# The order of TensorE's seven products per K pair: the products with t2 and t3 behind that with b22

## The chip, the cores and the metric

The kernel runs on one core of one Trainium2 chip. The metric is the device time of one execution in microseconds (us). The engines named below are TensorE (PE in the profile; PEld is its weight load, one ahead of each matmul), VectorE (DVE), ScalarE (ACT), GpSimd (POOL) and SyncE (SP, which only issues DMAs here).

## The reference

A trunk of two layers on x of 1 x 256 x 2048, in float32. Each layer is an attention part with two kinds of heads and a SwiGLU part, each between two RMS norms:

```python
for l in range(DEPTH):
    h = rms_norm(x, pre_mix_norm[l])
    m = hybrid_mixer(h, l, w_in[l], w_o[l], ...)     # h @ w_in, two attentions, @ w_o
    x = x + rms_norm(m, post_mix_norm[l])
    h = rms_norm(x, pre_ffn_norm[l])
    f = (silu(h @ w_gate[l]) * (h @ w_up[l])) @ w_down[l]
    x = x + rms_norm(f, post_ffn_norm[l])
```

w_in is 2048 x 6144, w_o 2048 x 2048, w_gate and w_up 2048 x 5632, w_down 5632 x 2048. The work around the change is these dense products of 256 tokens with the weights.

## The kernel before, in words

**Precision.** Each float32 operand is split into hi (rounded by ScalarE, line 307 or 279) and lo = value - hi (a subtraction on VectorE, line 317 or 281, for some weights on GpSimd, line 310). One product of two blocks is three matmuls into one PSUM bank: hi x hi, hi x lo, lo x hi (`product`, lines 1083 to 1086; a matmul there moves 512 columns against a stationary 128 x 128).

**Tiling.** K is walked in pairs (kp) of 2 x 128 rows, tokens in two halves of 128, columns in blocks of 512. For a pair and two blocks of columns the plain form needs eight block products, that is 24 matmuls (line 1250 in gate/up, lines 1356 to 1359 in down). In selected pairs the kernel uses a form with seven products instead (`seven_products`), 21 matmuls: sums of token blocks (s1 to s4, from `token_sums`) meet sums of weight blocks (t1 to t4), and four banks p1, p6, p7, q5 collect parts which `shared_part` (lines 1125 to 1129) adds to the four result banks at the end.

**How the sums of weights come about.** `mixed_weights` does it for each such pair from two weight tiles, G and T (T arrives with the first half of G added by an accumulating DMA of GpSimd, line 258). In program order: split of the whole T tile, which gives t1 and b22 together (hi on ScalarE, lo on VectorE, 128 x 1024); then on VectorE T<-T (line 290, 128 x 512: t2) and G<-G,T (line 291, 128 x 1024: t3 and t4); then the splits of t2 (Th<-T, Tl<-T, 128 x 512) and of t3 and t4 together (Th<-G, Tl<-G, 128 x 1024). In the profile's names, hi and lo of t1 and b22 are `hi` and `lo`, those of t2, t3 and t4 are `Th` and `Tl`.

**Where it is used.** In gate/up (eleven chunks c of 512 columns for each layer, eight pairs each) with two to five sevens in a chunk: chunk 0 has two, 1 has three, 2 and 10 four, 3 to 9 five, in the order kp 0, 2, 1, 3, 4, 5, 6, 7 with 2, 3, 4, 5, 6 as sevens. In down, in seven pairs of each half. In the input projection, pairs 4 and 5 of four of six column pairs, and in the output projection two pairs of its second half.

**What sets the order.** A scheduler places the instructions of each engine from the program order, priorities and its own estimate of when operands and buffers are ready; TensorE's matmuls, too, may stand elsewhere than the text has them. Each engine then runs its list in that order and waits at each instruction for what it needs. hi and lo have six buffers each, plain weight tiles (raw) four, G three, T four in gate/up; an instruction that fills a buffer waits for the last reader of its old content. SP issues the weight loads in one queue.

Of the kernel before, what the change touches and what calls it, by code (L numbers as in the profile page):

```python
# [167 lines left out]
def kernel(  # L168
# [30 lines left out]
    def four_banks(odd, names):  # L199
        makers = (bank, bank, bank, last_bank) if odd else (acc_bank,) * 4  # L200
        return [make(n) for make, n in zip(makers, names)]
# [143 lines left out]
    def weights(i, ahead):  # L345
        feed(i + 1 + ahead)
        return ready[i]
# [198 lines left out]
    def tick():  # L546
        clock[0] += 1
        for e in list(running):
            if e[0] <= clock[0]:
                try:  # L550
                    n = next(e[1])
                    e[0] = clock[0] + (PACE if n is None else n)
                except StopIteration:
                    running.remove(e)
# [508 lines left out]
    def seven_in(banks, extra, sums, xT, l, cc, kp, first, last):  # L1063
        hi, lo = weights(plan[l]["in"][cc[0], kp], LOOKAHEAD)
        m = weights(plan[l]["in"][cc[1], kp], LOOKAHEAD)
        seven_products(banks, extra, sums, *pair_blocks(xT, kp), hi, lo, m, first, last)
# [14 lines left out]
    def product(a, stat, moving, first, last):  # L1081
        sh, sl = stat
        hi, lo = moving
        nc.tensor.matmul(a, sh, hi, start=first, stop=False, skip_group_check=open_sums[0])  # L1084
        nc.tensor.matmul(a, sh, lo, start=False, stop=False, skip_group_check=open_sums[0])  # L1085
        return nc.tensor.matmul(a, sl, hi, start=False, stop=last, skip_group_check=open_sums[0])  # L1086
# [18 lines left out]
    def seven_products(banks, extra, sums, a11, a12, a22, hi, lo, m, first, last):  # L1105
        s1, s2, s3, s4 = sums
        p1, p6, p7, q5 = extra
        todo = (
            (p1, a11, (hi[:, 0, :], lo[:, 0, :]), first, last),
            (banks[0], a12, (hi[:, 1, :], lo[:, 1, :]), False, False),  # L1110
            (q5, s1, m["t1"], first, last),
            (p7, s3, m["t3"], first, last),
            (p6, s2, m["t2"], first, last),
            (banks[1], s4, m["b22"], False, False),
            (banks[2], a22, m["t4"], False, False),
        )
        for n, job in enumerate(todo):
            if n % 2 == 0:
                tick()
            newest_seven[0] = product(*job)  # L1120
# [14 lines left out]
    for l in range(L):  # L1135
# [27 lines left out]
        for kp in LATE_O:  # L1163
            i, j = (plan[l]["o"][c, kp] for c in (2, 3))
            if kp not in O_SEVEN:
                for c, i in ((2, i), (3, j)):
                    unit({t: accs[c, t] for t in range(NT)}, mix, i, kp, range(NT), kp == LATE_O[0], False)
                continue
            if kp == O_SEVEN[0]:
                extra = four_banks(False, [f"{q}_o{l}" for q in ("p1", "p6", "p7", "q5")])  # L1170
            hi, lo = weights(i, LOOKAHEAD)
            m = weights(j, LOOKAHEAD)
            seven_products(got, extra, forms[kp], *pair_blocks(mix, kp), hi, lo, m, kp == O_SEVEN[0], kp == O_SEVEN[-1])
            if kp == O_SEVEN[-1]:
                for t in range(NT):
                    mg[t, 1] = pool.tile([P, 2, CW], F32, tag="qk", bufs=4, name=f"mg_o{l}_{t}_1")
                shared_part(extra, [mg[t, 1][:, h, :] for t in range(NT) for h in range(2)])
                for c in (2, 3):
                    nc.vector.tensor_tensor(out=accs[c, 1], in0=accs[c, 1], in1=mg[1, 1][:, c - 2, :], op=shared_sign(1, c - 2))
# [72 lines left out]
        def seven(banks, extra, c, kp, first, last):  # L1252
            hi, lo = weights(plan[l]["gate"][c, kp], LOOKAHEAD)
            m = weights(plan[l]["up"][c, kp], LOOKAHEAD)
            e, o = xT[2 * kp], xT[2 * kp + 1]
            a11, a12, a22 = (e[:, 0, 0:P], e[:, 1, 0:P]), (o[:, 0, 0:P], o[:, 1, 0:P]), (o[:, 0, P:S], o[:, 1, P:S])
            seven_products(banks, extra, forms[kp], a11, a12, a22, hi, lo, m, first, last)

        for c in range(FF // CW):
            banks = four_banks(1 - c % 2, [f"c{q}_{l}_{c}" for q in ("11", "12", "21", "22")])  # L1260
# [62 lines left out]
        for half in range(2):  # L1323
# [74 lines left out]
            for t in range(NT):  # L1398
# [4 lines left out]
                for c in cc:  # L1403
                    for kp in range(nkp - tail, nkp):
# [4 lines left out]
                        for kk in range(2):  # L1409
                            sh, sl = jh[:, kk, t * P : (t + 1) * P], jl[:, kk, t * P : (t + 1) * P]  # L1410
                            last = kp == nkp - 1 and kk == 1
# [63 lines left out]
```

## Time and profile before

| | |
|---|---|
| median of 3 runs | 2189.1 us (2187.52 to 2189.52) |
| the profiled execution | 2189.0 us, of which its span is 2187.3 us |
| granted TensorE clock | 0.999 of full speed |
| ScalarE hi<-raw, 128 x 1024 | 494 times, mean 1055 ns |
| VectorE lo<-raw, 128 x 1024 | 472 times, mean 1221 ns |
| VectorE G<-G,T | 124 times, mean 1219 ns |
| DMA | 470.96 MB, mean 215 GB/s |

How to read it: the profile is of one execution. Busy times of TensorE come from modelled ends, and neighbouring instructions overlap, so the distance between starts tells more than the busy share. A line of a time line gives start, length, engine, source line, operation, out<-in and shape, and in brackets the idle time before it with what ended it. A line of the view of waits gives who waited for whom, the sum, the count and the longest. Gate/up runs from about 395 to 850 us in layer 0 and from about 1483 to 1940 us in layer 1.

### The profile page before, as it was taken

To read this page: it belongs to the slowest core of one execution; us is meant where nothing else is said; L and a number is where in the kernel's file an instruction comes from. 1 tells how busy PE (TensorE), PEld (TensorE's weight loads), DVE (VectorE), ACT (ScalarE), POOL (GpSimd) and SP (SyncE) were. 2 spreads that over 40 slices of the span, in tenths; PEclk is the share of its full clock that TensorE was granted. 3 is DMA by queue.
4 is the path that set the end of the run, shared out by engine and by line. 5 is a ranking of instruction groups with operands and counts; after the bars stand their busy time and mean duration, and the time that the engine had idled before them with its cause. 6 is when DMAs were issued, how large, how long until landed. Compare 5 with 4: busy or idle time off the path is not lost.

```text
span 2187.3 us, 28757 instructions
## 1 busy us (share of the span) xinstructions
PE 2170.0 (99%) x9950; PEld 1782.2 (81%) x9950; DVE 1914.1 (88%) x2639; ACT 1393.4 (64%) x2083; POOL 251.1 (11%) x241
## 2 busy tenths in 40 slices
PE   9999999999999999999999999999999999999998
PEld 7888888788888888888878888887888888888886
DVE  7888658999999999989878886589999999999997
ACT  7666665766666656666665656657566666666664
POOL 2100000031221220000010000001212212200000
PEclk9999999999999999999999999999999999999999
DMA  9545554587887876767465555555878877767683
GB/s 324 194 163 174 192 189 168 184 291 234 243 261 222 234 228 228 231 216 255 146 241 174 181 176 182 193 170 184 292 226 255 249 222 231 239 216 233 207 265 101
DMA packets 140563, 470.96 MB, mean 215 GB/s; under 512 B 15984, under 2 KB 17008, under 8 KB 139904
## 3 DMA queue, kind: packets, MB, share of 16 engines
q1 hardware_dynamic: 121952, 436.03, 57.7%
q0 software_dynamic: 17888, 32.55, 8.9%
q8 instruction: 78, 1.28, 0.2%
q10 hardware_dynamic: 576, 0.54, 0.1%
q14 instruction: 69, 0.57, 0.1%
HBM read 460.67 MB, written 8.39 MB: 214 GB/s over the span
## 4 chain that ended last, share of the span: by engine, by line
PE 87%; DVE 7%; issue 2%; DMA 2%; ACT 1%; SPq 0%; DVEq 0%; ACTq 0%
PE c L1250 16%; PE in L1084 7%; PE in L1086 7%; PE in L1085 7%; PE dn L1356 4%; PE dn L1357 4%; PE dn L1359 4%; PE p L1085 2%; PE c L1086 2%; PE c L1084 2%; PE c L1085 2%; PE p L1086 2%; PE p L1084 2%; PE o L569 2%; PE o L570 2%
## 5 line engine op out<-in xcount | busy, mean ns | idle before, releaser
L317 DVE TENSOR_TENSOR lo<-raw,hi 128x1024 fp32r<-128x1024 f32 x472 | 567.8, 1221 | 99.0 <-ACT hi L307 97.9
L307 ACT ACTIVATE hi<-raw 128x1024 fp32r<-128x1024 f32 x494 | 509.8, 1055 | 144.2 <-PE c L1086 36.8
L1250 PE MATMUL c<-hi,xF 128*128 128x512 f32 x1280 | 346.0, 391 | 0.1
L1250 PEld LDWEIGHTS c<-hi,xF 128*128 128x128 f32 x1280 | 238.3, 188 | 49.1 <-DVE xF L493 0.6
L258 POOL DMA_DIRECT2D T<-in_weights_in_turn_dram x124 | 108.8, 877 | 1343.6 <-DMA T<-in_weights_in_turn_dram 764.8
L1250 PE MATMUL c<-lo,xF 128*128 128x512 f32 x640 | 198.2, 390 | 2.5 <-DVE lo L317 2.5
L1356 PE MATMUL dn<-hi,jh 128*128 128x512 f32 x432 | 168.2, 389 | 0.0
L1357 PE MATMUL dn<-lo,jh 128*128 128x512 f32 x432 | 168.1, 389 | 0.0
L307 ACT ACTIVATE hi<-G 128x1024 fp32r<-128x1024 f32 x124 | 131.1, 1057 | 52.1 <-DMA G<-in_weights_in_turn_dram 20.8
L281 DVE TENSOR_TENSOR Tl<-G,Th 128x1024 fp32r<-128x1024 f32 x124 | 151.2, 1220 | 14.5 <-ACT Th L279 14.5
L279 ACT ACTIVATE hi<-T 128x1024 fp32r<-128x1024 f32 x124 | 130.3, 1051 | 51.0 <-PE c L1086 29.8
L279 ACT ACTIVATE Th<-G 128x1024 fp32r<-128x1024 f32 x124 | 130.8, 1055 | 47.8 <-DVE G L291 47.5
L281 DVE TENSOR_TENSOR lo<-T,hi 128x1024 fp32r<-128x1024 f32 x124 | 156.5, 1262 | 2.9 <-ACT hi L279 2.4
L291 DVE TENSOR_TENSOR G<-G,T 128x1024 f32<-128x1024 f32 x124 | 151.2, 1219 | 2.1
L1250 PEld LDWEIGHTS c<-lo,xF 128*128 128x128 f32 x640 | 120.1, 188 | 28.2 <-DVE lo L317 3.0
L317 DVE TENSOR_TENSOR lo<-G,hi 128x1024 fp32r<-128x1024 f32 x106 | 129.2, 1219 | 12.2 <-ACT hi L307 12.0
L1359 PE MATMUL dn<-hi,jl 128*128 128x512 f32 x432 | 133.0, 389 | 0.0
L1084 PE MATMUL in<-hi,xT 128*128 128x512 f32 x328 | 131.4, 402 | 0.5 <-ACT hi L889 0.5
L279 ACT ACTIVATE Th<-T 128x512 fp32r<-128x512 f32 x124 | 78.2, 631 | 83.6 <-DVE T L290 82.9
L1084 PE MATMUL in<-hi,xI 128*128 128x512 f32 x328 | 131.1, 401 | 0.0
L1085 PE MATMUL in<-lo,xI 128*128 128x512 f32 x328 | 128.0, 390 | 0.3 <-DVE lo L317 0.3
L1086 PE MATMUL in<-hi,xI 128*128 128x512 f32 x328 | 127.9, 391 | 0.0
(485 smaller groups left out, 4917.7 us busy)
## 6 DMA issues: line engine op xcount, KB each, us to landing
raw<-in_weights_in_turn_dram SPq DMA_DIRECT2D x494, 512.0 KB, 4.6
T<-in_weights_in_turn_dram SPq DMA_DIRECT2D x124, 512.0 KB, 5.5
G<-in_weights_in_turn_dram SPq DMA_DIRECT2D x124, 512.0 KB, 5.6
T<-in_weights_in_turn_dram POOLq DMA_DIRECT2D x124, 256.0 KB, 5.7
GU<-in_weights_in_turn_dram SPq DMA_DIRECT2D x32, 512.0 KB, 6.2
V<-in_weights_in_turn_dram SPq DMA_DIRECT2D x8, 512.0 KB, 3.9
away_ffn<-x SPq DMA_DIRECT2D x8, 512.0 KB, 7.4
xd<-away_ffn SPq DMA_DIRECT2D x8, 512.0 KB, 9.5
```

What stands on the lines that cost most here:

```text
L279: nc.scalar.activation(h, w, AF.Copy)
L281: newest_rest[i] = nc.vector.tensor_tensor(out=l, in0=w, in1=h.bitcast(F32), op=ALU.subtract)
L291: nc.vector.tensor_tensor(out=g, in0=g, in1=t2.unsqueeze(1).to_broadcast([P, 2, CW]), op=ALU.add)
L307: nc.scalar.activation(hi, raw, AF.Copy)
L317: rest = nc.vector.tensor_tensor(out=lo, in0=raw, in1=hi.bitcast(F32), op=ALU.subtract)
L1084: nc.tensor.matmul(a, sh, hi, start=first, stop=False, skip_group_check=open_sums[0])
L1085: nc.tensor.matmul(a, sh, lo, start=False, stop=False, skip_group_check=open_sums[0])
L1086: return nc.tensor.matmul(a, sl, hi, start=False, stop=last, skip_group_check=open_sums[0])
L1250: nc.tensor.matmul(a, stat[part], w[j][:, kk, :], start=first and kk + n == 0, stop=last and kk == 1 and n == 2)
L1356: nc.tensor.matmul(accs[c, t], sh, hi[:, kk, :], start=first, stop=False, skip_group_check=open_sums[0])
L1357: nc.tensor.matmul(accs[c, t], sh, lo[:, kk, :], start=False, stop=False, skip_group_check=open_sums[0])
L1359: nc.tensor.matmul(accs[c, t], sl, hi[:, kk, :], start=False, stop=last, skip_group_check=open_sums[0])
```

## The change

In `seven_products` the list of seven products is put in another order. Before, q5 (t1) is followed by p7 (t3), p6 (t2), banks[1] (b22) and banks[2] (t4); after, by banks[1], p6, p7 and banks[2]. The products themselves, their banks and their first and last marks stay.

```diff
             (q5, s1, m["t1"], first, last),
+            (banks[1], s4, m["b22"], False, False),
+            (p6, s2, m["t2"], first, last),
             (p7, s3, m["t3"], first, last),
-            (p6, s2, m["t2"], first, last),
-            (banks[1], s4, m["b22"], False, False),
             (banks[2], a22, m["t4"], False, False),
```

Because the scheduler works from this order, the lists of ScalarE, VectorE and SP change in places as well; GpSimd's list is the same.

## The prediction

> **What bounds the kernel now.** I read the page first, then busy times by stretches, then who waits for whom on the weight-load queue (PEld), then time lines of one chunk.
>
> ```profile
> span 2187.3 us, 28757 instructions
> PE 2170.0 (99%) x9950; PEld 1782.2 (81%) x9950; DVE 1914.1 (88%) x2639; ACT 1393.4 (64%) x2083; POOL 251.1 (11%) x241
> ```
>
> TensorE bounds it, but its 99% is made of modelled ends that overlap. What TensorE loses must be read from the starts of the weight loads: one precedes each matmul. The time line of one stalled pair (gate/up chunk 4 of layer 0, kp 5), from the last load of q5:
>
> ```profile
> 594.28 0.19 PEld L1086 LDWEIGHTS q<-hi,sl 128*128 128x128 f32 x1
> 594.51 0.41 PEld L1084 LDWEIGHTS p<-Th,sh 128*128 128x128 f32 x2
> 594.96 0.19 PEld L1085 LDWEIGHTS p<-Tl,sh 128*128 128x128 f32 x1
> 595.19 0.19 PEld L1086 LDWEIGHTS p<-Th,sl 128*128 128x128 f32 x1
> 595.42 0.19 PEld L1084 LDWEIGHTS c<-hi,sh 128*128 128x128 f32 x1
> 595.64 0.19 PEld L1085 LDWEIGHTS c<-lo,sh 128*128 128x128 f32 x1
> 596.25 0.19 PEld L1085 LDWEIGHTS p<-Tl,sh 128*128 128x128 f32 x1 [0.42 <-DVE Tl L281]
> 596.36 0.19 PEld L1086 LDWEIGHTS p<-Th,sl 128*128 128x128 f32 x1
> 596.60 0.19 PEld L1086 LDWEIGHTS c<-hi,sl 128*128 128x128 f32 x1
> ```
>
> Undisturbed starts stand 0.227 us apart (594.96 to 595.64: three steps, 0.68). From 595.64 to 596.60 there are three steps in 0.96, so this stall cost 0.28, which is its idle time of 0.42 less 0.14: 0.04 is the gap between any two loads, 0.10 is caught up by the next load at 596.36. The order seen is already not the one in the text: the scheduler has put p7's Tl product behind p6's three and two of b22's, and it still waits. All such waits:
>
> ```profile
> PEld p L1085 <- DVE Tl L281: 11.3, 20, 1.2
> PEld p L1084 <- ACT Th L279: 2.1, 6, 0.7
> PEld p_in L1085 <- DVE Tl L281: 0.4, 1, 0.4
> ```
>
> That is 13.8 us idle in 27 places, so 13.8 - 27 x 0.14 = **10.0 us** of lost TensorE time: the most that this change can remove. The Trainium skill (TensorE: Matmul & The Clock Gate, section "Architectural detail: the array is 16x 32x32, not 1x 128x128") says that TensorE's queue can pull weight loads ahead of matmuls in flight; if that hid these waits the 10.0 would be nothing. The trace shows only 0.10 per stall caught up, so the rest counts.
>
> The second engine is near its end too. One chunk, then the sum over 14 of them (chunks 3 to 9 of both layers):
>
> ```profile
> 643.60:684.80 41.20, 41.20 (x187) 33.98 (x186) 40.10 (x45) 26.75 (x32) 9.24 (x7) 1.00 0.78 237
> sum 582.00, PE 578.60 PEld 475.35 DVE 560.69 ACT 373.67 POOL 125.78; mean PE 41.33 PEld 33.95 DVE 40.05 ACT 26.69 POOL 8.98
> ```
>
> The columns are stretch, length, then PE, PEld, DVE, ACT, POOL. A chunk takes 582.0/14 = 41.57 on average, of which VectorE works 40.05. The one shown runs in 41.20 at a granted clock of 1.00: that is about what TensorE needs.
>
> **The change, part by part.** No instruction is added or removed; in each of 144 pairs (96 of gate/up, 28 of down, 16 of the input and 4 of the output projection) the six matmuls of p6 and p7 let the three of b22 pass, and p7 lets p6 pass. What the pair needs is made in the order t1 and b22 (one split), t2, then t3 and t4 (one split). The new order of use, t1, b22, t2, t3, t4, is that order. Three effects follow.
>
> *First, TensorE asks later.* The built order (in which the scheduler places the instructions on each engine; it holds no times) after q5 is now b22 x3, p6 x3, p7 x3. Counted in places after q5's last load, the first Th product goes from place 1 to 4, which is 3 x 0.227 = 0.68 later. Where the scheduler had deferred p7's Tl product (chunks 3 to 9) it goes only from 7 to 8, 0.23 later; where it had not (chunk 1), from 5 to 8.
>
> *Second, VectorE's built order changes with it.* Its time line for the same pair, before:
>
> ```profile
> 592.64 0.68 DVE L281 TENSOR_TENSOR Tl<-T,Th 128x512 fp32r<-128x512 f32 x1
> 593.25 0.68 DVE L290 TENSOR_TENSOR T<-T 128x512 f32<-128x512 f32 x1
> 593.85 1.22 DVE L317 TENSOR_TENSOR lo<-raw,hi 128x1024 fp32r<-128x1024 f32 x1
> 594.98 1.22 DVE L281 TENSOR_TENSOR Tl<-G,Th 128x1024 fp32r<-128x1024 f32 x1
> 596.12 1.22 DVE L291 TENSOR_TENSOR G<-G,T 128x1024 f32<-128x1024 f32 x1
> 597.26 0.68 DVE L281 TENSOR_TENSOR Tl<-T,Th 128x512 fp32r<-128x512 f32 x1
> 597.86 2.35 DVE L317 TENSOR_TENSOR lo<-raw,hi 128x1024 fp32r<-128x1024 f32 x2
> 600.13 1.22 DVE L281 TENSOR_TENSOR Tl<-G,Th 128x1024 fp32r<-128x1024 f32 x1
> ```
>
> The stalled product waited for the Tl that begins at 594.98 and ends at 596.2. In chunks 3 to 9 of the changed kernel the lo ahead of it (593.85) stands behind the next Tl<-T, and the two lo at 597.86 behind the last Tl<-G. Steps are 1.14 for 128x1024 (594.98 to 596.12) and 0.60 for 128x512. So Tl<-G can begin at 593.85 and end at 595.1; TensorE asks at 594.28 + 8 x 0.227 = 596.1. **The stall goes, with 1.0 us to spare.** What is late next? The three lo belong to kp 7 and to the next chunk; they end at about 597.9, 600.1 and 601.3, and kp 7 begins after 602. The shared part behind them begins when it did, because the sum of work ahead of it is the same.
>
> *Third, TensorE gives hi back six places earlier*, and this is what the second effect needs. ScalarE:
>
> ```profile
> 592.21 1.06 ACT L307 ACTIVATE hi<-raw 128x1024 fp32r<-128x1024 f32 x1 [1.03 <-PE c L1086]
> 593.18 1.04 ACT L279 ACTIVATE Th<-G 128x1024 fp32r<-128x1024 f32 x1
> 597.25 1.06 ACT L307 ACTIVATE hi<-raw 128x1024 fp32r<-128x1024 f32 x1 [1.56 <-PE c L1086]
> 598.22 1.04 ACT L279 ACTIVATE Th<-G 128x1024 fp32r<-128x1024 f32 x1
> ```
>
> Both hi<-raw wait for b22's last product, and the Th<-G that VectorE needs stands behind each. Released 6 x 0.227 = 1.36 earlier, the first hi starts about 1.0 earlier (ScalarE's own work ends 1.03 earlier), its Th<-G as soon as the G sum that ends where VectorE's row 592.64 begins is written and ends near 593.8. The second starts at 595.7, its Th<-G near 596.7 instead of 598.22. VectorE then idles nowhere.
>
> DMA issues: SP's built list has two G loads ahead of raw loads that they stood behind. A G waits for the Tl<-G above, which is earlier; the raw loads wait for the lo that moved, up to 2.9 later (593.85 to 596.7). They feed kp 1 of the next chunk, which stands 69 matmuls (24 + 24 + 21) or 15.7 us behind the start of kp 7. I cost this at nothing; the cover is that distance. POOL's list is unchanged. In the input and output projections one or two lo now stand inside the shared part, 1.14 each, so its banks return later: bounds 0 to 10 x 1.14 = 11.4 us; I take 0, because no wait of TensorE for these sums exceeds the row of 0.2 below. Down: no Tl row there waits at all, 0.
>
> ```profile
> PEld o L569 <- DVE o L1179: 0.3, 2, 0.2
> ```
>
> The sum, by groups of waits (same view, in windows; each line is us, times, longest):
>
> ```profile
> PEld p L1085 <- DVE Tl L281: 2.9, 6, 0.8
> PEld p L1085 <- DVE Tl L281: 4.2, 6, 1.0
> PEld p L1085 <- DVE Tl L281: 0.9, 2, 0.6
> PEld p L1084 <- ACT Th L279: 0.3, 1, 0.3
> PEld p L1085 <- DVE Tl L281: 1.3, 2, 1.0
> PEld p L1084 <- ACT Th L279: 0.6, 2, 0.3
> PEld p L1085 <- DVE Tl L281: 1.2, 1, 1.2
> PEld p L1084 <- ACT Th L279: 0.7, 1, 0.7
> PEld p L1085 <- DVE Tl L281: 0.2, 1, 0.2
> PEld p L1085 <- DVE Tl L281: 0.3, 1, 0.3
> PEld p L1084 <- ACT Th L279: 0.2, 1, 0.2
> ```
>
> - Chunks 3 to 8 (first line layer 0, second layer 1): 7.1 in 12, a loss of 7.1 - 12 x 0.14 = 5.4. All of it goes; the longest, 1.0, is under 1.14 + 0.23.
> - Chunks 1 and 2 (lines 3 and 4 layer 0, 5 and 6 layer 1): 3.1 in 7, loss 2.1. Th waits (0.3) fall under 0.68. Chunk 2's Tl has one lo fewer ahead (1.14) and goes. Chunk 1 keeps VectorE's order; its Tl product moves 0.68 against idle of 0.6 and 1.0, so about 0.3 stays. Gain 1.8.
> - Chunk 9 (lines 7 and 8 layer 0, 9 layer 1): 2.1 in 3, loss 1.7. The Th wait of 0.7 moves 0.68; the Tl wait of 1.2, after it, gains 1.14 + 0.23 but TensorE also comes 0.6 earlier, so about 0.2 stays. Gain 1.5.
> - Input projection 0.4, loss 0.3, moved six places: gain 0.3.
> - Chunk 0 (last two lines, layer 0; layer 1 has the same): 1.0 in 4, loss 0.4, stays: there p6's Tl is late, and it keeps its place.
>
> Sum: 5.4 + 1.8 + 1.5 + 0.3 = **9.0 us**. The profiled execution took 2189.0 (its span 2187.3 and 1.7 around it), the median of the runs is 2189.1: forecast **2180.0**.
>
> **Rivals.**
> *A, VectorE is the bound.* 40.05 of 41.57 is 96%, TensorE's loads 33.95 of 41.57 are 82%: a removed stall only shows up at the next product that reads a Tl, and the time stays near 2189. The Trainium skill (Perfetto Trace Analysis, section "Identifying the Most-Contended Engine") judges VectorE by occupancy and TensorE by its weight loads, which gives this result. Against it: the chunk of 41.20 has VectorE at 40.10, so 1.1 is free.
> *B, the place alone.* If VectorE's Tl does not come earlier, chunks 3 to 8 gain 0.23 in 11 stalls and 0.1 in the least, 2.6; with about 0.8 in chunk 9, 1.1 in chunk 1 and 0.3 in the input, 4.8: 2184.2. This is also the case that the text's order does little because the scheduler had made it already.
> *C, slower: VectorE starves behind ScalarE.* If ScalarE's two Th<-G kept their times (end 594.2 and 599.3), VectorE, with the lo no longer ahead, would idle 0.45 and 0.95 more, 1.4 per chunk. A chunk would need 40.05 + 1.4 and 0.3 to 1.0 of its other idle time, 41.8 to 42.5: 0.2 to 0.9 over 41.57, in 14 chunks 3 to 13, less 2 gained elsewhere: 2190 to 2200, middle 2195. It decides at the second hi<-raw: C holds if it starts after 597, not at 595.7.
>
> **How the numbers follow.** A measurement tells about 0.2%, 4.4 us, from no change. Forecast (2178 to 2183) 0.58; B 0.14, half of it beyond 0.2%; A 0.11; C 0.13; 0.04 for more gain, as the whole 10.0 and earlier buffers. Faster 0.58 + 0.04 + 0.07 = 0.69, same 0.07 + 0.11 = 0.18, slower 0.13. The range takes in all but C and the lowest: 2177.5 to 2189.5.
>
> **What would show it.** Right: the Tl and Th waits of PEld fall from 27 to under 10, those of chunk 0 remain, Tl<-G stands ahead of the lo<-raw, and the 14 chunks take 41.2 each. Wrong: waits for lo at L1250 (lo moved too far), DVE idle before Tl<-G for ACT Th (C), or equal chunk times with new waits (A).

## The result and the profile after

| | before | after |
|---|---|---|
| median of 12 runs each, us | 2188.86 (2187.29 to 2190.99) | 2183.77 (2182.70 to 2185.63) |
| ratio, 95% interval | | 0.9976, 0.9968 to 0.9985 |
| span of the profiled execution, us | 2187.3 | 2181.9 |

The kernel is 5.1 us faster (5.4 between the two profiled spans); forecast were 9.0. The 2183.8 lies 0.8 above the 2178 to 2183 that had most of the chance, and inside the stated range only because that takes in rivals A and B as well. The first lines of the page after:

```profile
span 2181.9 us, 28776 instructions
PE 2166.4 (99%) x9950; PEld 1783.2 (82%) x9950; DVE 1913.6 (88%) x2639; ACT 1394.8 (64%) x2083; POOL 258.8 (12%) x241
```

Every engine runs as many instructions as before, and VectorE and ScalarE are busy as long to within 1.4 us. GpSimd is busy 7.7 longer, nearly all of it in its lo<-G (51.6 instead of 43.6); I have not followed that further. What changed above all are the waits. Whom TensorE's weight-load queue waited for after the change (us, times, longest):

```profile
PEld p L1085 <- DVE Tl L281: 2.7, 8, 0.8
PEld c L1250 <- DVE xF L493: 2.0, 2, 1.0
PEld pT_df L823 <- DVE w L1127: 1.9, 4, 0.6
PEld q L1084 <- DVE act L1309: 1.6, 4, 0.5
PEld p L1084 <- ACT Th L279: 0.4, 2, 0.2
```

The waits for Tl and Th fell from 13.8 us in 27 places to 3.1 in 10, and the one in the input projection is gone. The largest rows that are new or longer: TensorE now waits 2.0 for xF, the first operand of gate/up (before: 0.6 in 2), 1.9 for L1127 in the input projection, and 1.6 for a bank that VectorE evicts late (q).

Where the 5.4 went can be read from stretches. Gate/up, from its first weight load (L1250) to that of down, before and then after (stretch, length, then PE, PEld, DVE, ACT, POOL):

```profile
sum 927.60, PE 920.97 PEld 756.37 DVE 889.68 ACT 603.02 POOL 183.30; mean PE 460.48 PEld 378.19 DVE 444.84 ACT 301.51 POOL 91.65
```

```profile
395.75:855.00 459.25, 457.96 (x2063) 378.75 (x2064) 444.33 (x543) 302.41 (x386) 94.73 (x68) 1.00 0.76 236
1480.95:1941.68 460.73, 458.95 (x2063) 378.48 (x2064) 445.34 (x543) 301.95 (x386) 96.29 (x68) 1.00 0.77 237
sum 919.98, PE 916.91 PEld 757.24 DVE 889.67 ACT 604.36 POOL 191.02; mean PE 458.46 PEld 378.62 DVE 444.84 ACT 302.18 POOL 95.51
```

Gate/up gained 7.6 (927.60 to 919.98), and 2.2 were given back outside it. Its first load in layer 0 begins at 395.75 instead of 394.81, 0.9 later; and from the end of gate/up in layer 0 to its start in layer 1 it now takes 625.95 instead of 624.71, 1.2 longer.

**The pair that the prediction followed** (chunk 4 of layer 0, kp 5). VectorE and then TensorE, after:

```profile
593.13 0.69 DVE L290 TENSOR_TENSOR T<-T 128x512 f32<-128x512 f32 x1
593.74 1.23 DVE L281 TENSOR_TENSOR Tl<-G,Th 128x1024 fp32r<-128x1024 f32 x1
594.88 1.22 DVE L291 TENSOR_TENSOR G<-G,T 128x1024 f32<-128x1024 f32 x1
596.02 0.69 DVE L281 TENSOR_TENSOR Tl<-T,Th 128x512 fp32r<-128x512 f32 x1
```

```profile
593.61 0.19 PEld L1086 LDWEIGHTS q<-hi,sl 128*128 128x128 f32 x1
593.84 0.19 PEld L1084 LDWEIGHTS c<-hi,sh 128*128 128x128 f32 x1
595.20 0.19 PEld L1084 LDWEIGHTS p<-Th,sh 128*128 128x128 f32 x1
595.42 0.19 PEld L1085 LDWEIGHTS p<-Tl,sh 128*128 128x128 f32 x1
```

Tl<-G follows T<-T with no lo between, and p7's Tl product, eighth after q5's last load, is loaded at 595.42 without a wait. That Tl's row ends at 594.97, so some 0.45 are to spare. ScalarE, which decides about rival C:

```profile
592.65 1.06 ACT L279 ACTIVATE Th<-G 128x1024 fp32r<-128x1024 f32 x1 [0.63 <-DVE G L291]
593.93 0.63 ACT L279 ACTIVATE Th<-T 128x512 fp32r<-128x512 f32 x1 [0.23 <-DVE T L290]
594.47 1.99 ACT L307 ACTIVATE hi<-raw 128x1024 fp32r<-128x1024 f32 x2
596.37 1.04 ACT L279 ACTIVATE Th<-G 128x1024 fp32r<-128x1024 f32 x1
```

Neither hi<-raw waits for b22's last product any more, and the second Th<-G starts at 596.37 (596.7 forecast, 598.22 before).

**The hand-over from the output projection to gate/up.** ScalarE there, before and after:

```profile
381.43 1.06 ACT L307 ACTIVATE hi<-raw 128x1024 fp32r<-128x1024 f32 x1 [3.87 <-PE o L571]
```

```profile
382.35 1.06 ACT L307 ACTIVATE hi<-raw 128x1024 fp32r<-128x1024 f32 x1 [5.05 <-PE o L571]
```

This hi waits for a buffer that TensorE gives back, and it does so 0.92 later. VectorE's rows tell why, first before and then after (rows are left out at the dots):

```profile
376.64 1.23 DVE L317 TENSOR_TENSOR lo<-raw,hi 128x1024 fp32r<-128x1024 f32 x1
...
378.98 1.29 DVE L1179 TENSOR_TENSOR o<-o,mg_o 128x512 f32<-128x512 f32 x2
```

```profile
375.19 0.68 DVE L1126 TENSOR_TENSOR mg_o<-p_o,mg_o 128x512 f32<-128x512 f32 x1
375.79 1.21 DVE L317 TENSOR_TENSOR lo<-raw,hi 128x1024 fp32r<-128x1024 f32 x1
376.92 0.68 DVE L1127 TENSOR_TENSOR mg_o<-p_o,mg_o 128x512 f32<-128x512 f32 x1
377.52 1.22 DVE L317 TENSOR_TENSOR lo<-raw,hi 128x1024 fp32r<-128x1024 f32 x1
...
379.85 1.28 DVE L1179 TENSOR_TENSOR o<-o,mg_o 128x512 f32<-128x512 f32 x2
383.44 2.59 DVE L317 TENSOR_TENSOR lo<-raw,hi 128x1024 fp32r<-128x1024 f32 x2 [2.31 <-ACT hi L307]
```

Two lo<-raw now stand inside the shared part, where before one did, and the sums on the banks o_2_1 and o_3_1 (L1179) are ready 0.87 later. The scheduler therefore put nine products on the bank o_2_0 ahead of the twelve on o_2_1 and o_3_1, where before it put five (e8 tests that the two lo are the reason). The first of the twelve is loaded here, before and after:

```profile
379.73 0.19 PEld L569 LDWEIGHTS o<-hi,mix_sb 128*128 128x128 f32 x1 [0.15 <-DVE o L1179]
```

```profile
380.59 0.19 PEld L569 LDWEIGHTS o<-hi,mix_sb 128*128 128x128 f32 x1
```

The twelve end the use of two hi buffers, which come back 4 x 0.227 = 0.91 later; hi, lo, the sums of L589, x and xF are all later by that, and gate/up with them.

### The profile page after: what moved, and what is told of

Its sections match the earlier page's. It is cut to its first block, busy times and chain, and to the rows that moved or that the text cites. A ratio compares the mean times of both kernels' runs of the same rounds, so it can differ in the third digit from the quotient of the medians.

```text
span 2181.9 us, 28776 instructions
## 1 busy us (share of the span) xinstructions
PE 2166.4 (99%) x9950; PEld 1783.2 (82%) x9950; DVE 1913.6 (88%) x2639; ACT 1394.8 (64%) x2083; POOL 258.8 (12%) x241
## 3 DMA queue, kind: packets, MB, share of 16 engines
q8 instruction: 78, 1.28, 0.2%
## 4 chain that ended last, share of the span: by engine, by line
PE 92%; DVE 4%; ACT 2%; issue 1%; DMA 1%; SPq 0%; DVEq 0%; ACTq 0%
PE c L1250 18%; PE in L1084 7%; PE in L1086 7%; PE in L1085 7%; PE dn L1356 4%; PE dn L1357 4%; PE dn L1359 4%; PE p L1085 3%; PE c L1085 3%; PE p L1086 3%; PE c L1084 3%; PE c L1086 3%; PE p L1084 3%; PE o L569 2%; PE o L571 2%; PE o L570 2%
## 5 line engine op out<-in xcount | busy, mean ns | idle before, releaser
L1250 PE MATMUL c<-hi,xF 128*128 128x512 f32 x1280 | 345.8, 391 | 1.5 <-DVE xF L493 1.5
L1250 PEld LDWEIGHTS c<-hi,xF 128*128 128x128 f32 x1280 | 238.3, 188 | 50.3 <-DVE xF L493 2.0
L1250 PE MATMUL c<-lo,xF 128*128 128x512 f32 x640 | 198.1, 390 | 2.5 <-DVE lo L317 2.5
L1250 PEld LDWEIGHTS c<-lo,xF 128*128 128x128 f32 x640 | 120.1, 188 | 28.1 <-DVE lo L317 3.0
```

The source lines that it names most:

```text
L1250: nc.tensor.matmul(a, stat[part], w[j][:, kk, :], start=first and kk + n == 0, stop=last and kk == 1 and n == 2)
```

## The experiments

Theory 1: in gate/up the mechanism and sizes of the prediction hold, and the projections (input and output) give back what I costed at nothing. Rivals: B, the place alone does it (its 2184.2 lies nearest to the result); that VectorE's order alone does it; that the swap of t2 and t3 counts by itself. The kernel before was measured anew beside the experiments; its medians there lie between 2188.3 and 2189.5, so a difference between medians of two kernels is uncertain by about half a microsecond.

**The projections as before** (e1).

```diff
-            seven_products(got, extra, forms[kp], *pair_blocks(mix, kp), hi, lo, m, kp == O_SEVEN[0], kp == O_SEVEN[-1])
+            seven_products(got, extra, forms[kp], *pair_blocks(mix, kp), hi, lo, m, kp == O_SEVEN[0], kp == O_SEVEN[-1], True)
...
+        if old:
+            todo = todo[:3] + (todo[5], todo[4], todo[3]) + todo[6:]
```

(the call of the input projection likewise)

> The new product order in gate/up and down only; the input and output projections keep the order of before. Theory 1 (the projections give back time that the prediction costed at 0): between the changed kernel and this one the hand-over from the output projection to gate/up loses 0.89 and 0.91 in the two layers and the input projection 0.3 in each, less the 0.29 of the one stall that went there: 2.1 in all, so 2183.8 - 2.1 = 2181.7, within 2181.0 to 2182.5, and the matrix products of gate/up start when they did before (394.8). Rival 2 (the losses there are absorbed further on, or belong to where the trace was cut): the same as the changed kernel, 2183.8 within 0.5.

Measured 2181.64 (ratio to before 0.9965, 0.9953 to 0.9978), 2.1 under the changed kernel, as theory 1 has it (2.6, if each is taken against the kernel before beside it). By its trace the hand-over is back to its length of before, though this execution reached it later, so that gate/up starts at 396.48 and not at 394.8. Its gate/up, where every engine has the list of the changed kernel:

```profile
sum 918.60, PE 916.01 PEld 757.88 DVE 889.45 ACT 607.16 POOL 187.01; mean PE 458.01 PEld 378.94 DVE 444.72 ACT 303.58 POOL 93.51
```

That is a gain of 9.0 where the changed kernel's execution shows 7.6.

**Which lo: those of the hand-over held back** (e8). `held` is the kernel's own list that queues the next lo<-raw behind an instruction.

```diff
-                shared_part(extra, [mg[t, 1][:, h, :] for t in range(NT) for h in range(2)])
+                part = shared_part(extra, [mg[t, 1][:, h, :] for t in range(NT) for h in range(2)])
...
-                    nc.vector.tensor_tensor(out=accs[c, 1], in0=accs[c, 1], in1=mg[1, 1][:, c - 2, :], op=shared_sign(1, c - 2))
+                    part = nc.vector.tensor_tensor(out=accs[c, 1], in0=accs[c, 1], in1=mg[1, 1][:, c - 2, :], op=shared_sign(1, c - 2))
+                held[:] = part, 2
```

> The changed kernel, with the two lo<-raw that went into the output projection's shared part held behind its last sum (L1179). All else in VectorE's list is that of the changed kernel; the built order then puts the 12 products on o_2_1 and o_3_1 ahead of nine on o_2_0, so their hi come back 9 x 0.227 = 2.0 us earlier than in the changed kernel, 1.1 earlier than in before. Theory 1 (the hand-over is set by that return of hi: hi<-raw, lo, L589, L627, transposes, gate/up): gate/up starts at least 0.9 earlier than in the changed kernel in each layer, up to 2.0 if nothing else on the chain is late: 2183.8 - 1.8 = 2182.0 down to 2179.8. Rival 2 (the loss there comes from the product order itself, not from the lo): no change in the hand-over, 2183.8 within 0.7. Rival 3 (the held lo are late for o_3_0): waits for lo at L570 and a time above 2184.

Measured 2182.60 (0.9969, 0.9956 to 0.9981), 0.6 above theory 1's upper end. Its hand-over is as long as that of before, 0.9 shorter per layer than in the changed kernel. The profiled spans differ by 2.4 (2179.5 against 2181.9), the medians by 1.2. Here the product order is the new one and only the two lo moved, so the loss of the hand-over came through them. Why nothing beyond the state of before was gained, its trace tells:

```profile
380.48 1.07 ACT L307 ACTIVATE hi<-raw 128x1024 fp32r<-128x1024 f32 x1 [3.05 <-DVE lo L317]
```

```profile
384.56 0.69 DVE L589 TENSOR_TENSOR mg_o<-o,mg_o 128x512 f32<-128x512 f32 x1 [0.40 <-PE o L571]
387.28 0.69 DVE L589 TENSOR_TENSOR mg_o<-o,mg_o 128x512 f32<-128x512 f32 x1 [0.55 <-PE o L571]
```

The hi comes 1.9 earlier than in the changed kernel, but now waits for VectorE's lo, and L589 waits for the last products on o, which come later in turn. So two other limits stood just behind the first.

**Both together, the input projection as before** (e11): the call of the input projection takes the old order, the hold of e8 is added.

> New order in gate/up, down and the output projection, the two lo<-raw of its hand-over held behind its last sum; the input projection keeps the order of before. Theory 1 (the parts add): 2181.6 of the kernel with the projections as before, less 0 to 1.1 per layer from hi that comes back earlier than in before: 2179.4 to 2181.6. Rival 2 (the hand-over has another limit just behind, and gives nothing over before): 2181.6 to 2182.2.

Measured 2181.78 (0.9966, 0.9954 to 0.9979): in rival 2's range and 0.2 above theory 1's, no better than e1's 2181.64. These two are the best of the versions measured, 7.7 us under the kernel before.

**The place alone** (e7). The new order everywhere, but in chunks 3 to 8 VectorE's list is that of before; `then(a, b)` puts a behind b on their engine; TlG5, TlG6 are the Tl<-G of the pairs kp 5 and kp 6, lo_a, lo_b, lo_c the lo<-raw of gate kp 7, up kp 7 and the next chunk's first gate block. Not shown is a line that keeps the G<-G,T of kp 6 behind the Tl<-G of kp 5; this and the next two experiments have it.

```diff
...
+        if i in fifth:
+            done["TlG5"] = newest_rest[i]
+        if i in sixth:
+            done["TlG6"] = newest_rest[i]
...
+            if i in lo_a:
+                then(done["TlG5"], rest)
+            if i in lo_c:
+                then(done["TlG6"], rest)
```

> The new product order everywhere, but VectorE's order in chunks 3 to 8 of gate/up is that of before: each lo<-raw ahead of the Tl<-G. ScalarE's list is that of the changed kernel. Theory 1 (both effects are needed): at kp 5 the Tl<-G ends near 596.0 and p7 asks at 595.4, so a stall of about 0.6 comes back in most chunks, and the 12 stalls lose 2.8 to 7: 2186.6 to 2190. Rival 2 (the prediction's B, the place alone makes the gain; its 2184.2 was nearest to the result): the same as the changed kernel, 2183.8 within 0.7, without Tl waits in chunks 3 to 8.

Measured 2187.31 (0.9993, 0.9984 to 1.0002), in theory 1's range and 3.5 above the changed kernel: B's place is not what made the 2183.8. ScalarE's list in these chunks is that of the changed kernel, and so is TensorE's but for one place in each, at kp 6, where a product with t4 now stands ahead of p7's Tl. The Tl waits of TensorE, then two of them in chunk 4:

```profile
PEld p L1110 <- DVE Tl L281: 9.8, 26, 0.7
```

```profile
596.35 0.19 PEld L1110 LDWEIGHTS p<-Tl,sh 128*128 128x128 f32 x1 [0.36 <-DVE Tl L281]
601.49 0.19 PEld L1110 LDWEIGHTS p<-Tl,sh 128*128 128x128 f32 x1 [0.29 <-DVE Tl L281]
```

What the later place spares at kp 5, TensorE waits for at kp 6, whose Tl<-G ends when it did. The twelve chunks (3 to 8 of both layers) took 498.7, before 498.3: nothing gained, where B had 2.6. Rival A's words describe this case, a stall that only shows up at the next Tl.

**VectorE's order alone** (e6). The order of products of before; in chunks 3 to 8 each lo<-raw stands behind the Tl<-G, as in the changed kernel (TlT6 is the Tl<-T of kp 6). VectorE's list there is then that of the changed kernel. The scheduler answered with other lists for ScalarE and TensorE too, so VectorE's order is not the only thing that differs from the kernel before.

```diff
...
+            if i in lo_a:
+                then(rest, done["TlT6"])
+                then(done["TlG6"], rest)
+            if i in lo_b:
+                then(rest, done["TlG6"])
```

> The product order of before everywhere, but VectorE's order in chunks 3 to 8 of gate/up is that of the changed kernel: each lo<-raw behind the Tl<-G that it stood ahead of. b22 is still last, so hi is given back late. Theory 1 (VectorE's order needs the earlier return of hi: ScalarE's Th<-G stands behind a hi<-raw that waits for b22): Th<-G ends at 594.2 and 599.3 as before, VectorE idles 0.4 and 1.0 ahead of the Tl<-G, and the scheduler moves p7's Tl product up again, so at most half of the 5.4 is gained: 2186 to 2190. Rival 2 (VectorE's order alone does it): the stalls of chunks 3 to 8 go, 2183.5 to 2185. Rival 3 (the prediction's C, VectorE starves): above 2190.

Measured 2208.44 (1.0087, 1.0073 to 1.0100), outside what theories 1 and 2 allowed; rival 3 has the direction. But VectorE idled for want of Th little longer than before (6.4 us instead of 5.2 in layer 0's gate/up); above all it was busy longer, 1933.8 instead of 1914.1. The page, a VectorE row, and GpSimd's at that time:

```profile
PE 2178.4 (99%) x9950; PEld 1778.9 (81%) x9950; DVE 1933.8 (88%) x2639; ACT 1391.0 (63%) x2083; POOL 257.3 (12%) x241
```

```profile
697.09 3.54 DVE L281 TENSOR_TENSOR Tl<-G,Th 128x1024 fp32r<-128x1024 f32 x1 [0.26 <-ACT Th L279]
```

```profile
696.82 2.72 POOL L318 TENSOR_TENSOR lo<-raw,hi 128x1024 fp32r<-128x1024 f32 x1
```

A Tl<-G of 1.22 took 3.54: GpSimd's lo runs to 699.54, and the Tl ends at 700.63, 1.09 after that. The Trainium skill (SBUF — State Buffer, section "SBUF: two separate sides") says that VectorE and GpSimd share a port pair that is locked for a whole instruction, and that the loser blocks fully; the two rows agree. GpSimd's second lo of a chunk stands where VectorE is to be at the eviction, one of whose operands lies in PSUM (before: L1303 at 693.47, two in 1.28 us beside GpSimd's lo at 693.38). A VectorE that is late meets it with a Tl instead.

**GpSimd held behind the Tl** (e9), to tell the collision from the late Th.

`beside` names, for GpSimd's second lo of a chunk (3 to 9), the pair at the chunk's start whose last split it has to wait for. In gate/up the order of every engine's list is that of e6.

```diff
+                elif i in beside:
+                    tc.add_manual_dep(rest.ins, newest_rest[beside[i]].ins.name, AFTER, reason="the shared port")
```

> The kernel with VectorE's order alone (2208.4), and GpSimd's second lo<-raw of chunks 3 to 9 held behind the Tl<-G of the pair at the chunk's start; TensorE's, VectorE's, ScalarE's and GpSimd's lists are the same, only SP's differs in a few loads. In the trace of 2208.4 VectorE was 19.7 us longer busy than in before (1933.8 against 1914.1), in single Tl instructions of 2.7 to 3.8 us that begin while that lo<-raw runs on GpSimd (696.82, 2.72 us; Tl<-G 697.09, 3.54 us). Theory 4 (VectorE, late by a fraction of a microsecond, falls beside GpSimd's work, and this makes the 20 us): VectorE's busy time returns to within 5 us of 1914, and the time to 2186 to 2192. Theory 1 as first put (the late return of hi through ScalarE makes it): above 2200 still, with Th waits of TensorE around 1 us.

Measured 2192.09 (1.0016, 1.0007 to 1.0025), 0.1 above theory 4's range: of 19.1 us over before 3.8 remain, so the collision made about 15. VectorE's busy time is back to within 2.9 us. Without the collision this kernel is still slower than before, and TensorE waits longer for ScalarE's Th (page, then the weight-load queue):

```profile
PE 2174.0 (99%) x9950; PEld 1780.5 (81%) x9950; DVE 1917.0 (87%) x2639; ACT 1391.3 (63%) x2083; POOL 257.4 (12%) x241
```

```profile
PEld p L1116 <- ACT Th L279: 8.8, 16, 1.6
```

Theory 1's reason (hi comes back late, Th with it) is not confirmed for this rest. Most of the Th waits in the row above stand at kp 5, and there the hi<-raw ahead of Th<-G had waited for no product. Th<-G itself waited, about 0.6 in most chunks, for VectorE's G<-G,T, and the way back from there (chunks 4 to 7 of layer 0) leads over VectorE's list to a hi<-G that waited 2.2 to 2.5 for its DMA. The chain of theory 1 is there at kp 6: in chunk 5 of layer 0 a hi<-raw waits 0.84 for b22's last product, Th<-G follows it, VectorE idles 0.22 for that, and TensorE 0.35 for the Tl, which ends at 642.96. But the scheduler had put p7's Tl product further ahead in this kernel, there to the fourth place behind q5's last load (641.79) from the ninth, where it would have been asked for at 643.83. I have not separated these causes.

**Only b22 moved** (e3) and **only the swap** (e4).

```diff
             (q5, s1, m["t1"], first, last),
+            (banks[1], s4, m["b22"], False, False),
             (p7, s3, m["t3"], first, last),
             (p6, s2, m["t2"], first, last),
-            (banks[1], s4, m["b22"], False, False),
```

> Only b22 is moved ahead; t3 stays ahead of t2. VectorE's list in gate/up is that of the changed kernel instruction for instruction; p7's Tl product is asked for three places, 0.68 us, earlier than there. Theory 1 (what the change brings is VectorE's order and b22's place): in the changed kernel the Tl<-G that p7 waits for ends 0.5 us ahead of the request at kp 5 and 1.3 ahead at the next pair (chunk 4), so 0.2 is short at most once per chunk and nearly nothing is lost: 2184 to 2186. Rival 2 (the swap of t2 and t3 carries half of it or more): 2186.5 or above, with Tl waits in most chunks.

Measured 2186.80 (0.9989, 0.9980 to 0.9998): rival 2's side, by 0.3, but without its sign: Tl waits stand in four of the twelve chunks 3 to 8, as in the changed kernel. The profiled spans differ by 3.0 (2184.9 against 2181.9). The trace splits it: gate/up 921.4 against 920.0, so 1.4 there; gate/up starts 0.9 later in layer 0, and what lies between the two gate/up is 0.6 longer. I had left the projections out. In the shared part the sum with p6 (L1126) stands first, and here p6 is done three places (0.68) later than in the changed kernel, which would fit; I have not tested it. The 1.4 of gate/up are not in chunks 3 to 8 (494.2 against 494.0). 1.2 of them lie in chunks 0 and 1: in chunk 1, where VectorE's order stays that of before, p7's Tl product stands at its old fifth place behind q5's last load and waits 0.57 and 1.15 in the two layers (before: 0.56 and 1.01), while in the changed kernel, at the eighth place, it waits 0 and 0.52.

```diff
             (q5, s1, m["t1"], first, last),
-            (p7, s3, m["t3"], first, last),
             (p6, s2, m["t2"], first, last),
+            (p7, s3, m["t3"], first, last),
             (banks[1], s4, m["b22"], False, False),
```

> Only t2 and t3 change places; b22 stays behind both. VectorE's list in gate/up is that of before. Theory 1 (the swap is worth something only as a later place of p7's Tl product behind b22): p7's Tl product is asked for at the same place as in before (seventh), the stalls stay, 2188.5 to 2190. Rival 2 (the swap carries its part of the gain by itself, as the 3.0 between the changed kernel and the one with b22 alone suggests): 2185.5 to 2187.

Measured 2189.26 (1.0000, 0.9991 to 1.0009): no effect, theory 1. By the medians the swap is worth 3.0 behind b22 (2.6, if each is taken against the kernel before beside it) and nothing ahead of it.

## Why the prediction was right in direction and too large

- *Asks later, VectorE earlier, hi back earlier* (the three effects in gate/up): right, and neither engine's order does it alone. In chunks 3 to 8 (from one chunk's first transposition to the next's, both layers) the place alone, which brings hi back earlier too, loses 0.3; VectorE's order alone, freed of GpSimd and with the lists that the scheduler then built for the other engines, loses 3.1; together they gain 4.3. The later place and the earlier hi were not taken apart. The sums of the twelve chunks before and after:

```profile
sum 498.33, PE 495.98 PEld 407.67 DVE 480.74 ACT 321.93 POOL 109.89; mean PE 41.33 PEld 33.97 DVE 40.06 ACT 26.83 POOL 9.16
```

```profile
sum 494.01, PE 493.56 PEld 408.02 DVE 477.93 ACT 323.15 POOL 118.14; mean PE 41.13 PEld 34.00 DVE 39.83 ACT 26.93 POOL 9.84
```

- *The terms of the sum.* "Chunks 3 to 8: 5.4" measured 4.3 in the changed kernel, and 5.5, 5.5 and 5.4 in e1, e8 and e11, whose lists there are the same. All of gate/up, forecast 8.7, measured 7.6, 9.0, 8.4 and 8.9. The size was right; single executions differ by over 1 us. In the changed kernel's, the longest Tl wait (0.82, at 1763.96) follows a G that came late from memory: ScalarE's hi<-G waited 2.77 for its DMA there. That chain is read from one trace and not tested.
- *"The stall goes, with 1.0 us to spare"*: it went, with 0.45. I counted the place from q5's load of before (594.28), but a TensorE that loses less also comes earlier (593.61).
- *"I take 0, because no wait of TensorE for these sums exceeds the row of 0.2"* is **the step that failed**. I had seen that lo would stand inside the shared part and looked for a direct wait for the sums. The sums' lateness acted one step on: it changed the order that the scheduler built for the products behind, and through it the return of two hi buffers. It cost 0.9 per layer at the hand-over. The input projection lost 0.3 per layer, where TensorE's new waits are those for L1127 (1.9 in 4, in the list above). That is 2.4, less the stall of 0.3 won there: 2.1, which e1 confirmed. The bounds that I gave, 0 to 11.4, held it; the 0 that I took did not. So the 8.7 of gate/up became 7.6 and the 0.3 of the projections became -2.1: 5.5, the 5.4 of the spans.
- *Down, and chunk 0:* as forecast, 0 (462.2 and 462.3 us for both layers' down, from its first weight load to its last) and unchanged.
- *What would show it:* Tl and Th waits in 10 places (under 10 was asked, two of layer 0's and layer 1's chunk 0 each among them), no waits for lo at L1250 beyond two that before has as well, chunks 3 to 8 of 41.0 to 41.8, and 41.2 as the mean of chunks 3 to 9.
- *Rival A* fell for the change as a whole: VectorE's work is unchanged, 444.8 per layer in gate/up, and the chunks got shorter. *B* had the nearest time by chance: its own case, made, gives 2187.3. *C's* condition did not come (both hi<-raw of the pair are done between 594.47 and 596.46); the kernel with VectorE's order alone, which keeps b22 last, has it: there that hi<-raw starts at 597.32, after a wait of 1.08 for b22's last product.

## What to carry to other kernels

A reordering under a scheduler has to be costed where its lists change, not only where its reason lies: follow each moved instruction to the buffers whose return it shifts, in every stage that shares the function. When two engines' orders change together, try each alone before crediting one; in chunks 3 to 8 neither gained anything by itself. And let a shared function take its order from the caller if stages want different ones: new in gate/up and down, old in the projections was as good as any version measured.

## What the runs showed of the hardware that I had not expected

A GpSimd tensor_tensor of 2.6 to 2.7 us made VectorE instructions with both operands in SBUF wait to its end: 1.22 became 3.54, and the 128x512 Tl of 0.68 took up to 3.68. In all seven such meetings of a Tl in e6 (chunks 6 to 9), VectorE's instruction ended 1.09 (128x1024) or 0.56 (128x512) after GpSimd's. These meetings and their consequences made about 15 us of a 2190 us kernel. The kernels before and after the change have some too, in gate/up outside chunks 3 to 9: five lo of VectorE that take 2.0 to 2.6 us before, four of 2.5 to 4.0 after. Without stalls, a chunk takes 41.01 to 41.04 (e1, nine of the twelve of chunks 3 to 8), 0.2 below the 41.20 that the prediction took for what TensorE needs.
